# Mixer B of an encoder layer: queries sorted by class, one preparation stage, and TensorE in program order

## The chip, the cores and the metric

The kernel runs on one core of one Trainium2 chip. The metric is the device time of one execution in microseconds (us), lower is better. A core has TensorE (PE: matmuls; PEld: loads of their stationary operands), VectorE (DVE), ScalarE (ACT), GpSimdE (POOL), SyncE (SP, which here only issues transfers) and 16 DMA engines. Each engine works its own instructions off in order; semaphores tie the engines together.

## What is computed

One layer of an encoder over 1024 tokens of width 1024, in float32:

```
u = RMSNorm(x);  [qA|kA|vA|qB|kB|vB] = u @ w_in
oA = RMSNorm(global GQA of qA,kA,vA)              # mixer A, 8 query heads
oB = RMSNorm(mixture of 3 dilated windows)        # mixer B, 8 heads of 64
h = x + concat(oA, oB) @ w_out
h = h + HierarchicalMoE(RMSNorm(h))               # 32 experts
y = RMSNorm(h)

# mixer B, for window, dilation in ((128,1), (512,4), (2048,16)):
#   query t attends t + j*dilation for |j*dilation| <= window/2
#   outputs of the three are merged by their softmax denominators
```

## The kernel before

**Stages.** The input projection runs first and mixer A's attention is mixed into it; mixer A's rest follows, with the first heads of mixer B beside it; then comes mixer B, with the half of the output projection that needs only mixer A; then the other half with the router; then 32 experts one after the other; then the final norm. Expert weights stream in from HBM through 39 buffers of 512 KB ("units"), 14 of which lie where mixer B's tiles (`keep`) lay before.

**Mixer B.** Scores are kept transposed, keys on partitions and queries along the free axis. The dilations 4 and 16 are handled together by class: a class is the tokens with equal t mod 4, so there are 4 classes of 256 tokens, and each class needs two key tiles of 128 by 256 queries (`front_c`, `back_c`). The window of dilation 1 is handled in 8 key tiles of 128 by 256 queries, two per step (`front_w`, `back_w`). A head so has 8 steps. The front of a step is four matmuls into a bank of `ps_b` (keys high and low parts against queries, lines 705 and 706 for classes, 731 and 732 for windows), then `masked`: DVE adds the mask (line 691), ACT takes the exponential and rounds it to `ph`, POOL subtracts to get the low part `pl` (line 696). The back is six matmuls of the values with `ph` and `pl` (lines 718 to 721, 758 to 760), then an add into the head's output `ob` (line 762). After a head's last back `divided` transposes `ob`, divides by the denominator and writes `o_b`. In the class fronts both the keys `k2[:, ks]` (the stationary operand) and the queries `q2[:, c::4]` (the moving operand) are read with a step of four elements.

**Preparation.** Before a head's fronts its keys and queries are transposed on TensorE (`flipped`, line 303), and the row maximum of all scores is found. `prepare_b` does the flips and four class maxima (matmul line 642, DVE line 644), `finish_b` the maxima over windows (line 670, DVE line 673), brings the class maxima back to token order with four small matmuls (line 662), writes the negative maximum into the queries and flips them again to `q1`. These are two stages: while head h runs, head h+1 is finished and head h+2 prepared. Three sets of `k2`, `q2` and `q_st` are kept for it.

**Order.** `attend` writes a step as front, back of the step two before, three pieces of preparation. The output projection's first half (`first_half`, matmul line 827) advances by one piece per step. `tc` then schedules every engine by its own timeline, so that what stands on TensorE in mixer B is the scheduler's order; only the router stage and the experts hold TensorE to program order (`manual_schedule`). The first half needs the first four 128-row blocks of w_out, which come through one buffer (`raw`, line 800) and are split by ACT and DVE into `woh` and `wol`.

Of the kernel before, what the change touches and what calls it, by code (L numbers as in the profile page):

```python
# [22 lines left out]
P = 128  # L23
# [35 lines left out]
def _tables():  # L59
# [28 lines left out]

    band = []
    for j in (0, 1, 1, 7):  # L90
        near = np.abs((128 * j + p)[:, None] - (_window(j) + q)[None, :]) <= 64
        band.append(add(near.astype(int)))
# [33 lines left out]
def tile_encoder(ctx, tc, I, out):  # L126
# [171 lines left out]
    def flipped(dst, src, rows):  # L298

        for b in range(2):  # L300
            ps = bank("x", [P, 4, P], F32R)
            for i in range(4):
                T.transpose(ps[:rows, i], src[:, 4 * b + i], eyer)
            act(dst[:rows, 512 * b:512 * b + 512].rearrange("p (j i) -> p j i", j=4), ps[:rows])
            yield
# [142 lines left out]
    def attend(n, stages, steps, ahead, pace):  # L448
# [17 lines left out]
        waiting = []  # L466
        for h in range(n):
            coming = [stage(d - 1 - a, h + 1 + a) for a in range(d) if h + 1 + a < n]
            for front, back in steps(h, state.pop(h)):
                front()  # L470
# [11 lines left out]
        for back in waiting:  # L482
            back()
# [89 lines left out]
    sizes = [D] * 9 + [2 * NT * NQ, NT * NQ + 4 * P]  # L573
    keep = ExitStack()

    def spot(i):
# [3 lines left out]
    k_st, *pairs, q20 = [pools[i].tile([P, n], F32R, name=f"keep{i}") for i, n in enumerate(sizes[:-1])]  # L580
    q1b = pools[-1].tile([P, NT * NQ], F32R, name="q1b")
    back_m = pools[-1].tile([P, 4, P], F32, name="back")
    k2s = {2: pairs[0], 0: pairs[2], 1: pairs[5]}
    q2s = {2: pairs[1], 0: pairs[3], 1: pairs[6]}
    k1s = [t[0:66] for t in (pairs[4], pairs[7])]
    k_st = k_st.rearrange("p (t f) -> p t f", t=NT)
    q_st = {i: t.rearrange("p (t f) -> p t f", t=NT) for i, t in
            ((2, q20[:, 0:NT * NQ]), (0, q20[:, NT * NQ:2 * NT * NQ]), (1, q1b))}
# [6 lines left out]
    mask_c, mask_w = masks[:, 0:2], masks[:, 2:6]  # L595
    own = small[:, 60:64]
# [21 lines left out]
    def load_b(h):  # L618
        if h < 8:
            nc.sync.dma_start(k_st.bitcast(F32), bk_d[h])  # L620
            nc.sync.dma_start(q_st[h % 3][:, :, 0:192].bitcast(F32), bq_d[h])

    def prepare_b(h, _):
        k, q = k_st, q_st[h % 3]
# [7 lines left out]
        k2 = k2s[h % 3]  # L632
        yield from flipped(k2, k, P)
        q2 = q2s[h % 3]
        yield from flipped(q2, q[:, :, 0:128], P)
        load_b(h + 1)
        mc = qst2.tile([P, 4, 2], F32, name="mc", bufs=3)
# [9 lines left out]
        return k2, q2, mc  # L647

    def finish_b(h, state):
        k2, q2, mc = state  # L650
        q = q_st[h % 3]
        k1 = k1s[h % 2]
        nc.sync.dma_start(k1[0:64].bitcast(F32), k2[64:128].bitcast(F32))
        mw = qst2.tile([P, NT], F32, name="mw")
        junk = qst2.tile([P, 256], F32, name="junk", bufs=1)
# [4 lines left out]
        pm = bank("x", [P, 4, 2])  # L660
        for c in range(4):
            T.matmul(pm, back_m[:, c], mx[:, c], start=(c == 0), stop=(c == 3))
        m = qst2.tile([P, NT], F32, name="m")
        V.tensor_copy(m.rearrange("p (t i) -> p t i", t=2), pm.rearrange("p i t -> p t i"))
        yield
        for j0 in range(0, NT, 2):
# [8 lines left out]
            yield  # L675
        t = qst2.tile([P, NT], F32, name="negm")
# [5 lines left out]
        yield from flipped(q1, q[:, :, 128:194], 66)  # L682
        return k2, k1, q2, q1

    def steps_b(h, state):
# [3 lines left out]
        def masked(ps, mask):  # L689
            p = pp2.tile([P, 512], F32, name="p", bufs=2)  # L690
            V.tensor_tensor(p, ps.rearrange("p a b -> p (a b)"), mask.rearrange("p a b -> p (a b)"), op=OP.add)
            act(p, p, AF.Exp, scale=0.125)
            ph = pp2.tile([P, 512], F32R, name="ph", bufs=3)
            act(ph, p)
            pl = pp2.tile([P, 512], F32R, name="pl", bufs=3)
# [3 lines left out]
        def front_c(c):  # L699
            if c == 2:  # L700
                load_v(h, "w")
            ps = bank("b", [P, 2, 256])
            for t in range(2):
                ks = slice(512 * t + c, 512 * t + 512, 4)
                T.matmul(ps[:, t], k2[:, ks], q2[:, c::4], start=True, stop=False)
                T.matmul(ps[:, t], k1[:, ks], q1[:, c::4], start=False, stop=True)
            st["c", c] = masked(ps, mask_c)

        def back_c(c):
            if c == 0:  # L710
# [656 lines left out]
```

## Time and profile before

| | us |
|---|---|
| median of 3 runs (1396.47 to 1398.05) | 1397.87 |
| the profiled execution | 1393.38 |
| its span, which all rows below count in | 1391.7 |
| mixer B with the first half of the output projection | about 430 to 670 |
| output projection's second half, router | 670 to 780 |
| experts | 780 to 1360 |

PE is the engine that is busy nearly everywhere, and its granted clock is full except in short stretches. A matmul's duration counts its way through the array as well, so that matmuls overlap in the records; what one costs in a row of others is the distance of two starts.

### The profile page before, as it was taken

The page shows a single profiled execution, that of the slowest core. Times are in us where ns is not written, and L with a number is a line of the kernel's source. Part 1 is how long each engine was busy: PE and PEld are TensorE (multiplying, and loading weights), DVE is VectorE, ACT ScalarE, POOL GpSimd, SP SyncE. Part 2 cuts the span into 40 slices and gives each one's busy share as a digit, 9 for nine tenths or more (in the row PEclk, how much of TensorE's full clock was granted, in tenths as well). Part 3 has the DMA queues.
Part 4 walks back from the last instruction along what each step waited for, and adds up shares of the span by engine and source line. Part 5 has one row for each costly group of instructions (what it writes and reads, how often), then busy time and mean ns, then how long its engine had stood idle before and what let it go on. Part 6 is the DMA issues. An engine that isn't in the chain of part 4 may idle for free. (4 is left out here: it accounts for less than half of the span.)

```text
span 1391.7 us, 21904 instructions
## 1 busy us (share of the span) xinstructions
PE 1303.2 (94%) x7333; PEld 1110.6 (80%) x7333; DVE 1152.4 (83%) x2001; ACT 926.2 (67%) x1366; POOL 568.6 (41%) x556
## 2 busy tenths in 40 slices
PE   5999899999998999999897999999999999999983
PEld 5999779888976889889686788878888888888862
DVE  5788997899868777667587799989999999999976
ACT  5334556655566656556443688878888888888873
POOL 5673566745566645446354611122111111111215
PEclk9999999999998999899998999999999999999997
DMA  7113321231242564445767999999999999999925
GB/s 258 62 39 85 84 68 54 61 75 36 58 138 60 145 186 117 112 128 164 278 210 240 308 371 367 353 341 372 360 351 351 345 360 355 349 353 342 376 74 226
DMA packets 213044, 299.63 MB, mean 215 GB/s; under 512 B 94307, under 2 KB 115939, under 8 KB 212928
## 3 DMA queue, kind: packets, MB, share of 16 engines
q1 hardware_dynamic: 200528, 272.91, 58.1%
q0 software_dynamic: 11968, 24.55, 6.7%
q8 instruction: 58, 0.95, 0.3%
q10 hardware_dynamic: 432, 0.75, 0.3%
q14 instruction: 58, 0.48, 0.1%
HBM read 267.85 MB, written 44.58 MB: 224 GB/s over the span
## 5 line engine op out<-in xcount | busy, mean ns | idle before, releaser
L140 DVE TENSOR_TENSOR wl<-unit,wh 128x1024 fp32r<-128x1024 f32 x140 | 168.4, 1223 | 21.1 <-ACT wh L131 20.1
L1163 POOL DMA_INDIRECT o_b<-xn_d,rows x32 | 51.4, 1606 | 303.1 <-PE ps_a L1180 300.8
L131 ACT ACTIVATE wh<-unit 128x1024 fp32r<-128x1024 f32 x140 | 147.3, 1062 | 36.3 <-PE ps_b L1196 12.5
L529 POOL TENSOR_TENSOR psum<-psum,p 128x512 f32<-128x512 f32 x93 | 138.0, 1484 | 66.7 <-ACT p L131 56.6
L263 PE MATMUL ps_i<-wih,ul 128*128 128x256 f32 x576 | 163.1, 283 | 1.2 <-DVE ul L140 1.2
L261 PE MATMUL ps_i<-wih,uh 128*128 128x256 f32 x576 | 162.7, 283 | 0.8 <-ACT uh L131 0.8
L262 PE MATMUL ps_i<-wil,uh 128*128 128x256 f32 x576 | 162.2, 282 | 0.0
L131 ACT ACTIVATE ph<-p 128x512 fp32r<-128x512 f32 x192 | 119.0, 630 | 12.7 <-DVE pl L445 5.7
L445 DVE TENSOR_TENSOR pl<-p,ph 128x512 fp32r<-128x512 f32 x93 | 96.1, 1035 | 24.7 <-ACT ph L131 24.6
L131 ACT ACTIVATE p<-ps_b 128x512 f32<-128x512 f32 x128 | 74.6, 595 | 62.2 <-PE ps_b L519 39.7
L261 PEld LDWEIGHTS ps_i<-wih,uh 128*128 128x128 f32 x576 | 109.6, 190 | 7.0 <-ACT uh L131 1.5
L262 PEld LDWEIGHTS ps_i<-wil,uh 128*128 128x128 f32 x576 | 109.4, 190 | 5.5
L263 PEld LDWEIGHTS ps_i<-wih,ul 128*128 128x128 f32 x576 | 109.5, 190 | 5.1 <-DVE ul L140 1.7
L696 POOL TENSOR_TENSOR pl<-p,ph 128x512 fp32r<-128x512 f32 x64 | 83.4, 1309 | 73.2 <-ACT ph L131 51.9
L1233 POOL DMA_INDIRECT y_d<-y,rows x31 | 50.3, 1622 | 137.5 <-ACT y L131 134.2
L140 DVE TENSOR_TENSOR wl<-rawc,wh 128x1024 fp32r<-128x1024 f32 x70 | 84.4, 1223 | 10.4 <-ACT wh L131 9.9
L500 DVE TENSOR_REDUCE m<-ps_x 128x1 f32<-128x512 f32 x128 | 84.9, 678 | 7.9 <-PE ps_x L499 7.6
L1196 PE MATMUL ps_b<-wh,x_hi 128*128 128x512 f32 x256 | 87.0, 421 | 0.0
L131 ACT ACTIVATE wh<-rawc 128x1024 fp32r<-128x1024 f32 x70 | 74.3, 1067 | 18.2 <-PE ps_b L1196 7.2
L1220 PE MATMUL ps_d<-wh,h_hi 128*128 128x512 f32 x256 | 81.0, 397 | 1.7 <-ACT h_hi L131 1.7
L1220 PE MATMUL ps_d<-wh,h_lo 128*128 128x512 f32 x256 | 81.1, 398 | 1.5 <-DVE h_lo L140 1.5
L1196 PE MATMUL ps_c<-wh,x_hi 128*128 128x512 f32 x256 | 80.9, 397 | 0.0
(326 smaller groups left out, 3888.9 us busy)
## 6 DMA issues: line engine op xcount, KB each, us to landing
unit<-in_w_up SPq DMA_DIRECT2D x49, 512.0 KB
unit<-in_w_gate SPq DMA_DIRECT2D x47, 512.0 KB
unit<-in_w_down SPq DMA_DIRECT2D x44, 512.0 KB
rawc<-in_w_gate SPq DMA_DIRECT2D x25, 512.0 KB
rawc<-in_w_down SPq DMA_DIRECT2D x23, 512.0 KB
rawc<-in_w_up SPq DMA_DIRECT2D x22, 512.0 KB
h_b<-in_w_down SPq DMA_DIRECT2D x19, 512.0 KB
raw<-in_w_in SPq DMA_DIRECT2D x36, 256.0 KB
```

Of the source, the lines that this page charges most:

```text
L131: A.activation(o, i, f, **kw)
L140: (eng or V).tensor_tensor(lo, src, hi, op=OP.subtract)
L261: T.matmul(ps[:, jj], u_hi[j][:, k], wh, start=(k == 0 and jj == 0), stop=False, skip_group_check=True)
L262: T.matmul(ps[:, jj], u_hi[j][:, k], wl, start=False, stop=False, skip_group_check=True)
L263: T.matmul(ps[:, jj], u_lo[j][:, k], wh, start=False, stop=(k == 7), skip_group_check=True)
L445: engine("pl").tensor_tensor(pl, p, ph, op=OP.subtract)
L500: V.tensor_reduce(m2[:, j, b:b + 1], ps, axis=AX.X, op=OP.max)
L529: engine("s").tensor_tensor(st["s"], st["s"], p, op=OP.add)
L696: G.tensor_tensor(pl, p, ph, op=OP.subtract)
L1163: gathers.append(G.indirect_dma_start(out=x_g, out_offset=None, in_=xn_d[:, :], in_offset=bass.IndirectOffsetOnAxis(ap=rows, axis=0), boun ...
L1196: T.matmul(st["gu"[n % 2]], lhs[:, k % 4], rhs[:, 512 * a:512 * a + 512], start=(k == 0 and i == 0), stop=(k == 7 and i == 2))
L1220: T.matmul(py[b], lhs[:, k], w[n][:, 512 * b:512 * b + 512], start=(k == 0 and i == 0), stop=(k == 3 and i == 2))
```

## The change

Four things change, in mixer B and in what is mixed into it.

1. **Queries by classes.** After its flip, `q2` is copied by ACT into `q2c` with the four classes one after another (`classes`, `by_class`), and `q1` is flipped straight into that order. Class fronts read 256 queries that lie together; window fronts read four blocks of 64. The window masks, `ps` and `po` follow the same order, so that the DVE maxima over windows read their bank with a step of four, and the add into `ob` reads and writes `ob` with a step of four. The keys as stationary operand are read as before, and so are both operands of the class maxima.
2. **One stage.** `prepare_b` and `finish_b` become one; there are two sets of `k2`, `q2c`, `k1`, one `q2`, two `q_st`. The four small matmuls stand after the window maxima, and three empty pieces stand ahead of the flip of `q1`. The copy of `k2` to `k1` is issued right after the flip of `k2`. Eleven instead of 14 units lie where those tiles lay.
3. **More distance.** The back runs three steps after its front instead of two; `p` has 3 buffers, `ph` and `pl` have 4; `divided` runs some parts after the last back; the values of the windows are loaded one step later.
4. **TensorE by the program.** `attend(..., fine=True)` yields after every part (front, piece, back, piece, piece); the output projection advances once in 4.2 parts; the whole loop stands under `manual_schedule` for TensorE, while the other engines are scheduled as before. In `first_half` the norm of the next row (`normed`) and its transposes (`turned`) are apart.

```
-    def flipped(dst, src, rows):
+    def flipped(dst, src, rows, classed=False):
...
+            if classed:
+                act(classes(dst[:rows])[:, :, 128 * b:128 * b + 128], by_class(ps[:rows].rearrange("p j i -> p (j i)")))
...
+                if fine:
+                    waiting.append(back)
...
+                    def second():
+                        if len(waiting) > ahead:
+                            owing.extend([3, f] for f in waiting.pop(0)() or ())
+
+                    for part in (front, piece, second, piece, piece)[:2 + pace]:
+                        part()
+                        for o in owing:
+                            o[0] -= 1
+                        if owing and owing[0][0] < 0:
+                            owing.pop(0)[1]()
+                        yield
+                    continue
...
+        q2c = q2s[h % 2]
+        act(classes(q2c), by_class(q2))
...
-                V.tensor_tensor_reduce(junk, ps[:, t], mask_w[:, w], 1.0, NEG, op0=OP.add, op1=OP.max,
-                                       accum_out=mw[:, j0 + t:j0 + t + 1])
+                V.tensor_tensor_reduce(classes(junk), by_class(ps[:, t]), classes(mask_w[:, w]), 1.0, NEG,
+                                       op0=OP.add, op1=OP.max, accum_out=mw[:, j0 + t:j0 + t + 1])
...
+        for _ in range(3):
+            yield
+        yield from flipped(q1, q[:, :, 128:194], 66, True)
+        return k2, k1, q2c, q1
...
-            p = pp2.tile([P, 512], F32, name="p", bufs=2)
+            p = pp2.tile([P, 512], F32, name="p", bufs=3)
...
-                T.matmul(ps[:, t], k2[:, ks], q2[:, c::4], start=True, stop=False)
-                T.matmul(ps[:, t], k1[:, ks], q1[:, c::4], start=False, stop=True)
+                T.matmul(ps[:, t], k2[:, ks], q2[:, 256 * c:256 * c + 256], start=True, stop=False)
+                T.matmul(ps[:, t], k1[:, ks], q1[:, 256 * c:256 * c + 256], start=False, stop=True)
...
-                    V.tensor_tensor(o[:, b0:b0 + nb], o[:, b0:b0 + nb], po[0:65, 0:nb], op=OP.add)
+                    V.tensor_tensor(by_class(o[:, b0:b0 + nb]), by_class(o[:, b0:b0 + nb]), po[0:65], op=OP.add)
...
-    side = attend(8, [prepare_b, finish_b], steps_b, 2, 3)
+    side = attend(8, [prepare_b], steps_b, 3, 3, True)
...
+    with tc.manual_schedule(engines={mybir.EngineType.PE}):
+        for _ in side:
+            due += RATE_O / 4.2
```

TensorE around the first steps of a head, before: `L642` are class maxima, `L705` and `L706` class fronts, `L718` and `L720` a back.

```order
L642 MATMUL ps_x<-keep_5000,keep_5001 128x256 x2
L706 MATMUL ps_b<-q_5822,keep_5007 128x256
L705 MATMUL ps_b<-keep_5006,keep_5005 128x256
L706 MATMUL ps_b<-q_5822,keep_5007 128x256 x2
...
L718 MATMUL ps_i_6113<-ph,v_c 65x256
L720 MATMUL ps_i_6113<-ph,v_c 64x256
```

The same place after (`L678` class maxima, `L692` window maxima, `L735` and `L736` class fronts, `L789` to `L791` a back, `L861` the output projection, `L853` its transposes).

```order
L735 MATMUL ps_b<-keep_4999,keep_4998 128x256
L736 MATMUL ps_b<-q_5813,keep_5000 128x256
L735 MATMUL ps_b<-keep_4999,keep_4998 128x256
L736 MATMUL ps_b<-q_5813,keep_5000 128x256
L861 MATMUL ps_d<-woh,o_hi 128x512
L861 MATMUL ps_d<-wol,o_hi 128x512
L861 MATMUL ps_d<-woh,o_lo 128x512
L678 MATMUL ps_x<-keep_4995,keep_4994 128x256 x2
L789 MATMUL ps_i_6035<-ph,v_w 65x4x64
```

Where three class fronts stood in one row, one front is now followed by a product of the output projection, a maximum and a back.

TensorE at the end of mixer B, before: `L740` is `divided`, `L819` the transposes of the first row of the second half, `ps_x` the bank of its products.

```order
L827 MATMUL ps_d<-woh,o_lo 128x512
...
L740 MATMUL ps_i_8109<-mats,ob 128x65 x4
L740 MATMUL ps_i_8118<-mats,ob 128x65 x4
L819 MATMUL ps_b<-mats,on 128x128 x4
L827 MATMUL ps_x<-woh,o_hi 128x512
```

And after (`L770` is `divided`, `L853` those transposes):

```order
L791 MATMUL ps_i_8115<-pl,v_w 65x4x64
L770 MATMUL ps_i_8123<-mats,ob 128x65 x4
L770 MATMUL ps_i_8132<-mats,ob 128x65 x4
L861 MATMUL ps_d<-woh,o_hi 128x512
L861 MATMUL ps_d<-wol,o_hi 128x512
L861 MATMUL ps_d<-woh,o_lo 128x512
...
L853 MATMUL ps_b<-mats,on 128x128 x4
```

Five groups of three products of the first half now stand between the last division and those transposes; ahead of the division the backs of the last four steps stand, in four sixes, with one group of products after the first of them.

ScalarE in the preparation of a head, after: `p` and `ph` are the exponentials and their rounding, `keep_4994` is `q2`, `keep_4999` is `q2c`.

```order
L132 ACTIVATE keep_4994<-ps_x 128x512
L132 ACTIVATE ph<-p 128x512
L132 ACTIVATE keep_4994<-ps_x 128x512
L132 ACTIVATE p<-p 128x512
L132 ACTIVATE keep_4999<-keep_4994 128x1024
L132 ACTIVATE ph<-p 128x512
```

The copy of 1024 elements is new and stands between an exponential and its rounding.

## Rows read from the trace of the kernel before

**Rows 1.** The page: busy time by engine; granted clock in 40 slices.
```profile
PE 1303.2 (94%) x7333; PEld 1110.6 (80%) x7333; DVE 1152.4 (83%) x2001; ACT 926.2 (67%) x1366; POOL 568.6 (41%) x556
...
PEclk9999999999998999899998999999999999999997
```

**Rows 2.** Stretches from:to: length, busy us (instructions), granted clock, DMA share; mixer B, experts.
```profile
430.00:670.00 240.00, 229.39 (x1406) 206.28 (x1404) 173.79 (x497) 149.42 (x255) 123.85 (x118) 0.93 0.48 131
...
780.00:1360.00 580.00, 572.76 (x2639) 462.40 (x2637) 520.55 (x506) 482.18 (x564) 118.41 (x85) 1.00 0.96 337
```

**Rows 3.** The same view: one of six half-clock stretches of mixer B, and their sum.
```profile
575.10:585.40 10.30, 10.30 (x54) 9.88 (x54) 5.20 (x19) 6.34 (x12) 4.81 (x4) 0.50 0.21 45
...
sum 37.60, PE 37.14 PEld 34.68 DVE 23.38 ACT 21.40 POOL 18.12; mean PE 6.19 PEld 5.78 DVE 3.90 ACT 3.57 POOL 3.02
```

**Rows 4.** The same view: the longest stretch between two of these.
```profile
493.20:551.20 58.00, 55.45 (x352) 49.39 (x352) 43.76 (x122) 33.97 (x60) 25.29 (x28) 1.00 0.54 146
```

**Rows 5.** Timeline of PE, start us, us: class fronts before the clock fell at 575.1.
```profile
574.85 0.42 PE L706 MATMUL ps_b<-q,keep 66*128 66x256 f32 x1
575.08 0.43 PE L705 MATMUL ps_b<-keep,keep 128*128 128x256 f32 x1
575.32 0.42 PE L706 MATMUL ps_b<-q,keep 66*128 66x256 f32 x1
...
576.45 0.41 PE L718 MATMUL ps_i<-ph,v_c 128*65 128x256 f32 x1
576.66 0.41 PE L720 MATMUL ps_i<-ph,v_c 128*64 128x256 f32 x1
```

**Rows 6.** Timeline, all engines: window fronts at full clock.
```profile
585.62 0.28 PE L731 MATMUL ps_b<-keep,keep 128*128 128x256 f32 x1
...
585.74 0.29 PE L732 MATMUL ps_b<-q,keep 66*128 66x256 f32 x1
```

**Rows 7.** Timeline of PEld: two loads each; L670's operand lies together, L642's is stepped.
```profile
585.99 0.31 PEld L670 LDWEIGHTS ps_x<-keep,keep 128*128 128x128 f32 x2
...
587.96 0.55 PEld L642 LDWEIGHTS ps_x<-keep,keep 128*128 128x128 f32 x2
```

**Rows 8.** Groups by line in 430:670: count | busy us, mean ns | idle before, releaser.
```profile
L691 DVE TENSOR_TENSOR p<-ps_b,masks 128x512 f32<-128x512 f32 x64 | 43.9, 686 | 14.5 <-PE ps_b L706 7.4 <-POOL pl L696 4.4 <-PE ps_b L732 2.6
...
L705 PE MATMUL ps_b<-keep,keep 128*128 128x256 f32 x64 | 29.0, 453 | 3.0 <-DVE p L691 2.9
L673 DVE CUSTOM_DVE_ANT_0 junk<-ps_x,masks 128x256 f32<-128x256 f32 x64 | 26.9, 421 | 14.9 <-PE ps_x L670 12.9 <-PE ps_b L519 0.5
...
L131 ACT ACTIVATE ob<-ps_i 65x512 f32<-65x512 f32 x16 | 17.6, 1098 | 6.9 <-PE ps_i L721 6.7
...
L642 PEld LDWEIGHTS ps_x<-keep,keep 128*128 128x128 f32 x62 | 17.0, 322 | 0.5
L131 ACT ACTIVATE keep<-ps_x 128x512 fp32r<-128x512 f32 x28 | 16.5, 596 | 7.5 <-PE ps_x L303 7.3
...
L762 DVE TENSOR_TENSOR ob<-ob,ps_i 65x448 f32<-65x448 f32 x8 | 4.9, 607 | 0.0
```

**Rows 9.** Waits of PE in 430:670: us in total, times, longest.
```profile
PE ps_b L705 <- DVE p L691: 2.9, 2, 1.6
...
PE ps_x L662 <- DVE mx L658: 1.0, 2, 0.5
```

**Rows 10.** Timeline of PE at the end of mixer B.
```profile
669.68 0.47 PE L740 MATMUL ps_i<-mats,ob 65*128 65x65 f32 x4 [0.35 <-DVE ob L762]
672.68 0.66 PE L819 MATMUL ps_b<-mats,on 128*128 128x128 f32 x4 [2.54 <-DVE on L814]
...
676.69 0.80 PE L827 MATMUL ps_x<-woh,o_lo 128*128 128x512 f32 x1 [1.50 <-DVE o_lo L140]
```

**Rows 11.** Timeline of ACT: splits of the third and fourth block of w_out.
```profile
499.33 1.06 ACT L131 ACTIVATE woh<-raw 128x1024 fp32r<-128x1024 f32 x1 [1.00 <-DMA raw<-in_w_out]
505.48 1.05 ACT L131 ACTIVATE woh<-raw 128x1024 fp32r<-128x1024 f32 x1
```

More of the change, by code (lines that the diff above doesn't have):

```diff
@@ L91, in _tables @@
         near = np.abs((128 * j + p)[:, None] - (_window(j) + q)[None, :]) <= 64
-        band.append(add(near.astype(int)))
+        band.append(add(near.astype(int)).reshape(P, 64, 4).transpose(0, 2, 1).reshape(P, 256))
     masks = np.stack(cls + band, 1)
@@ L446, in weights, with attend @@
         return ph, pl
-    def attend(n, stages, steps, ahead, pace):
+    def attend(n, stages, steps, ahead, pace, fine=False):
         state, at = {}, {}
@@ L482, in attend @@
         for back in waiting:
-            back()
+            owing.extend([0, f] for f in back() or ())
+        for _, f in owing:
+            f()
     qst = att.enter_context(tc.tile_pool(name="qst", bufs=2))
@@ L579, in tile_encoder @@
     pools = [keep.enter_context(spot(i)) for i in range(len(sizes))]
[L580 to L585, printed above, removed]
+    k_st, q2, *pairs, q01 = [pools[i].tile([P, n], F32R, name=f"keep{i}") for i, n in enumerate(sizes)]
+    k2s, q2s, k1s = pairs[0::3], pairs[1::3], [t[0:66] for t in pairs[2::3]]
     k_st = k_st.rearrange("p (t f) -> p t f", t=NT)
-    q_st = {i: t.rearrange("p (t f) -> p t f", t=NT) for i, t in
-            ((2, q20[:, 0:NT * NQ]), (0, q20[:, NT * NQ:2 * NT * NQ]), (1, q1b))}
+    q_st = [q01[:, i * NT * NQ:(i + 1) * NT * NQ].rearrange("p (t f) -> p t f", t=NT) for i in range(2)]
     final = {}
@@ L672, in finish_b @@
                 w = 0 if j0 + t == 0 else 3 if j0 + t == NT - 1 else 1
-                V.tensor_tensor_reduce(junk, ps[:, t], mask_w[:, w], 1.0, NEG, op0=OP.add, op1=OP.max,
-                                       accum_out=mw[:, j0 + t:j0 + t + 1])
+                V.tensor_tensor_reduce(classes(junk), by_class(ps[:, t]), classes(mask_w[:, w]), 1.0, NEG,
+                                       op0=OP.add, op1=OP.max, accum_out=mw[:, j0 + t:j0 + t + 1])
             yield
+        pm = bank("x", [P, 4, 2])
+        for c in range(4):
+            T.matmul(pm, back_m[:, c], mx[:, c], start=(c == 0), stop=(c == 3))
+        yield
+        m = qst2.tile([P, NT], F32, name="m")
+        V.tensor_copy(m.rearrange("p (t i) -> p t i", t=2), pm.rearrange("p i t -> p t i"))
         t = qst2.tile([P, NT], F32, name="negm")
@@ L854, in first_half @@
                 V.tensor_tensor(h[:, j], ps, x[b], op=OP.add)
+                if b == 0 and j + 1 < NT:
+                    o = turned(on, "x")
+                yield
         split_out(4)
@@ L858, in tile_encoder @@
     more, due = first_half(), 0.0
-    for _ in side:
-        due += RATE_O
-        while due >= 1:
-            due -= 1
-            next(more, None)
-    run(more)
+    with tc.manual_schedule(engines={mybir.EngineType.PE}):
+        for _ in side:
+            due += RATE_O / 4.2
+            while due >= 1:
+                due -= 1
+                next(more, None)
+        run(more)
     names.update(a="b", b="x", c="d", d="i1", s="i0")
-    first_mixed = turned(o_b[0][:, 0], 1, "a")
+    first_mixed = turned(normed(o_b[0][:, 0], 1), "a")
     wka.close()
```

91 lines of the change are left out of this document (46 added, 45 removed).

## Prediction

> **What bounds the kernel now.** I read the page first, then the stretches, then inside mixer B the groups by line, the timeline and the waits. The page says that PE is busy for 94% of the span and that its clock is full but for some slices in the middle [rows 1]. In the experts PE is busy for 573 of 580 us at full clock [rows 2], so what is won or lost before them moves the end by about as much; the change touches nothing there. The work that changes lies in 430 to 670. There PE is busy for 229 of 240 us, but the clock is 0.93, and DVE is the second engine with 174 us, 72% [rows 2]. [...] PE's own waits are small: for a free bank `ps_b` 2.9 us, for the row maxima 1.0 [rows 9]. The tail is larger: from the last division at 669.68 to 676.69 PE waits 2.54 and 1.50 us for the norm of the first row of the next stage [rows 10]. So mixer B is nearly bound by PE, with DVE not far behind, and what can be won is the stepped reading, the half clock, these waits and the tail.
>
> **The change part by part.** All against the profiled execution of 1393.4 us; the median of the runs is 4.5 higher, which I add at the end.
>
> 1. *Queries that lie together.* 128 matmuls (L705 has 64 [rows 8], L706 as many) now have a moving operand without a step; their stationary operand, the keys, is stepped as before. If only the moving operand sets 0.235, they fall to 0.12: 128 x 0.115 = 14.7 us. But loads of stepped stationary operands are slow too: two take 0.55 together [rows 7] and one of them lasts 0.32 [rows 8], so the second starts some 0.22 behind the first; two that lie together take 0.31 [rows 7]. Four fronts in a row are then paced by their loads at 0.22. That gives 128 x 0.015 = 2 us, and a little more where the first load of a four hides behind the matmul ahead. I take -3 us, between 0 and -15.
>
> 2. *Clock.* At half clock a back's matmuls start 0.21 apart (576.45 to 576.66 [rows 5]) instead of about 0.12; stepped ones lose nothing. By counts, half clock does 54 matmuls in 10.3 us, 5.2 per us [rows 3], full clock 352 in 58, 6.1 per us [rows 4]: 37.6 us at the lower rate lose some 5 us; if nothing in them were stepped, half, 19. I hold 10 for near. In the new order a front stands between products of 512 columns and a back, so the long runs of slow columns that stood ahead of the fall are gone; the class maxima keep their steps, and new waits (5) may let the clock fall again. I take half of it back: -5, between 0 and -14.
>
> 3. *Waits that the new order is made around.* The maxima come back to token order after the window maxima, the flip of `q1` after three empty pieces, and the back a step later. The two waits, 2.9 + 1.0 = 3.9 us [rows 9], should nearly go: -3.5, between 0 and -3.9. What is late next is DVE.
>
> 4. *Tail.* Five groups of three products stand between the last division and the transposes of the next row; at 580 us / 2639 = 0.22 us each [rows 2] they are 3.3 us, which cover most of 2.54 + 1.50 [rows 10]. -3.5, between -2 and -4.
>
> 5. *TensorE in program order beside DVE.* The scheduler could put other matmuls ahead of one whose bank was not free; now PE waits. A head's eight maxima each cost DVE two instructions of 0.42 [rows 8], 0.84 us, and PE 0.24 to 0.47. They stand three to a step over about two and two thirds steps, beside the masks (0.69 a step [rows 8]), two adds of 0.6 [rows 8], the divisions and an add of the output projection: some 12 us of DVE against 10 us of PE. The three banks of `ps_x` let PE run ahead by about one piece; the rest, 1 us or a little more for each of seven heads, PE stands still, and behind the waiting matmul a front stands, and so ACT and POOL. +7, between 0 and +14.
>
> 6. *Stepped reading by DVE and ACT.* 64 maxima over windows read their bank with a step of four, 24 adds into `ob` read and write with it, ACT has one more copy of 1024 a head and reads the bank of `q1` with a step. No row shows DVE with a step. The nearest are the ACT writes of `ob` with a step of four, 1098 ns for 512, against 596 for `keep` without [rows 8]: 1.0 ns an element more. By that a maximum would cost 0.26 us more, 64 x 0.26 = 17 us of DVE just where (5) has it behind, and the adds 24 x 0.43 = 10 us. On the other side PE reads with the step at 0.235 / 256 = 0.92 ns an element, about as fast as a maximum takes its elements anyway (0.42 us for 256), so a read may cost nothing. I take reads at nothing and writes at the price of `ob`: 10 us of DVE spread over 24 places, where DVE is idle 28% of the time; a tenth shows, +1. The copy, 1.1 to 2.1 us of ACT a head by the same rows, lies behind fronts with three steps of slack: 0. Together +1, between 0 and +27.
>
> [...]
>
> 7. *w_out.* Its blocks pass one buffer, and the splits of the third and fourth stand 6.15 us apart (499.33, 505.48 [rows 11]). In program order the products that need blocks 2 to 4 stand two to four us apart on PE and can't be passed by other work. If the chain of loads starts as before, PE waits 2 to 6 us once, less what it would have waited for DVE anyway. +2, between 0 and +6.
>
> 8. *The rest at nothing:* the empty pieces, the copy to `k1` earlier on SP, the values of the windows a step later but used four steps after their load as before, the larger rings, and eleven early units, which like the fourteen fill while the router stage runs. If those came late, the first expert would wait, and DMA share above 0.96 [rows 2] shows that there is little to catch up with.
>
> Sum: -3 - 5 - 3.5 - 3.5 + 7 + 1 + 2 = -5 on 1393.4, so 1388.4, and with 4.5 added 1392.9. Items 2 and 5 are both rough, and a program order that is steady on PE lessens small losses that I priced nowhere: starts in 430 to 670 that come late by less than what the waits list. I give these 2.9 us more and forecast 1390.
>
> **The rivals.** *The gains all come:* the clock stays up (-14), the loads hide (-8), tail and waits go and DVE keeps pace (+2): about -25, 1373. For it: the falls came behind slow runs; against it: DVE at 72% has to do the same in less time. *Nothing:* the scheduler had hidden the stepped reading, the program order loses as much at DVE as it wins; 1398. That the change doesn't do what it says belongs here: the keys keep their step, and class fronts stay at 0.22. *Slower:* DVE pays for the step in PSUM. 64 maxima at +0.26 are 17 us in the place where PE waits for banks: 1390 - 1 + 17 = 1406. It decides from about +0.13 us each, where the gain is gone. For it: the `ob` rows; against it: PE's 0.92 ns.
>
> **How the numbers follow.** Forecast (1382 to 1394) 0.42, all gains (1366 to 1382) 0.19, nothing 0.16, slower (1401 to 1412) 0.23. A measurement of this kernel can tell about 0.2%, 2.8 us, from no change. Faster so is 0.42 + 0.19 = 0.61, same 0.16, slower 0.23. The range takes the forecast, nothing, most of the gains and the nearer half of the slower case: 1370 to 1406.
>
> **What would show it.** In the profile after: starts of class fronts 0.21 to 0.22 apart (near 0.12 says that loads don't count, 0.235 that nothing changed). Less than 25 us at half clock in mixer B; as much as before says that item 2 is wrong. A maximum over windows at 0.42 as before, or 0.55 and more, which is the slower rival. PE's waits for DVE on `ps_x` of 5 to 10 us in sum. Transposes of the next stage's first row within 1.5 us of the products ahead of them. First products of w_out with waits of some us for `woh`. The forecast falls if mixer B and the first half of the output projection don't end some 6 us earlier, or if the experts then wait for weights.

## The result, and the profile after

The changed kernel takes 1416.33 us, median of 4 runs (1412.85 to 1422.50); the kernel before 1397.17 in the same series. The ratio is 1.0152, 95% interval 1.0126 to 1.0178: some 21 us slower, where 1390 was forecast and 1406 was the upper end of the range. The profiled run took 1415.44 us.

First the page: span, PE's busy time, and the granted clock in 40 slices, to be laid beside [rows 1].
```profile
span 1413.8 us, 21932 instructions
...
PE 1310.6 (93%) x7333; PEld 1114.0 (79%) x7333; DVE 1162.6 (82%) x2001; ACT 942.3 (67%) x1374; POOL 565.7 (40%) x556
...
PEclk9999999999997699989999899999999999999997
```
The number of matmuls is the same. The thirteenth and fourteenth slice (424 to 495 us) stand at 0.7 and 0.6 where they stood at 0.8 and 0.9 before: mixer A ends there and mixer B begins in earnest. The stretches say the same, after and then before (from:to, length, busy us (instructions) of PE, PEld, DVE, ACT, POOL, clock, DMA share, GB/s):
```profile
428.00:470.00 42.00, 35.17 (x157) 26.23 (x157) 26.61 (x59) 27.41 (x48) 23.77 (x17) 0.78 0.13 38
470.00:505.00 35.00, 29.05 (x150) 26.32 (x150) 24.02 (x57) 19.14 (x32) 15.64 (x16) 0.66 0.54 146
...
560.00:620.00 60.00, 55.39 (x344) 50.60 (x343) 41.10 (x120) 37.41 (x61) 26.04 (x26) 0.91 0.43 111
...
428.00:698.00 270.00, 237.94 (x1414) 210.14 (x1415) 185.69 (x506) 164.88 (x267) 126.55 (x126) 0.89 0.43 118
...
800.00:1380.00 580.00, 572.83 (x2634) 463.29 (x2633) 521.30 (x507) 481.88 (x564) 116.80 (x81) 1.00 0.96 338
```
```profile
428.00:470.00 42.00, 39.20 (x220) 33.48 (x221) 31.87 (x84) 29.51 (x54) 27.02 (x20) 0.88 0.18 47
470.00:505.00 35.00, 32.27 (x210) 28.67 (x207) 27.20 (x75) 24.64 (x43) 18.84 (x20) 0.90 0.70 181
...
560.00:620.00 60.00, 56.49 (x341) 51.34 (x341) 41.17 (x128) 33.37 (x58) 27.42 (x27) 0.91 0.44 114
```
From 428 to 505 PE does 307 instructions where it did 430. The last division of mixer B begins at 690.19, 20.5 us behind [rows 10]; the two spans differ by 22.1. Nine groups of three products of the first half still stand behind it, where before the last of them had started at 667.98. So the first product of the second half starts at 698.99 instead of 674.02; the experts run as in [rows 2]. PE's timeline after, then before:
```profile
690.19 0.46 PE L770 MATMUL ps_i<-mats,ob 65*128 65x65 f32 x4 [0.56 <-DVE ob L793]
...
695.14 0.60 PE L853 MATMUL ps_b<-mats,on 128*128 128x128 f32 x4
...
698.99 0.39 PE L861 MATMUL ps_x<-woh,o_hi 128*128 128x512 f32 x1
```
```profile
674.02 0.73 PE L827 MATMUL ps_x<-woh,o_hi 128*128 128x512 f32 x1 [0.69 <-ACT o_hi L131]
```

PE's waits between 428 and 692 (us in sum, times, longest) have changed their kind. Over 428 to 698 they sum to 31.9 us against 15.4 before, 4.7 of which lie behind 670 in the next stage [rows 10]. The longest sums after:
```profile
PE ps_x L312 <- DVE keep L708: 5.9, 5, 1.9
PE ps_x L692 <- DVE mw L695: 4.2, 5, 1.6
PE ps_i L746 <- issue: 3.6, 2, 2.3
PE ps_d L573 <- DVE pl L457: 3.2, 6, 0.8
PE ps_x L700 <- DVE mw L695: 2.9, 3, 1.8
PE ps_d L861 <- ACT o_hi L132: 1.9, 1, 1.9
```
L312 is the flip of `q1`, which needs the negative maximum (L708); L692 a product whose bank a maximum (L695) still reads; L746 the first back of a class, L573 mixer A's back, L700 the product that brings the maxima to token order. The wait of [rows 9] for a free `ps_b`, 2.9 us, is gone. Behind such a wait the clock falls in some cases and not in others. In PE's timeline the wait of 1.61 us ends at 599.54, and the stretch from 599 to 611 has a clock of 0.57 (the nine us ahead: 1.00):
```profile
597.52 0.40 PE L692 MATMUL ps_x<-keep,keep 128*128 128x256 f32 x2
599.54 0.58 PE L692 MATMUL ps_x<-keep,keep 128*128 128x256 f32 x2 [1.61 <-DVE mw L695]
```
```profile
599.00:611.00 12.00, 10.57 (x50) 9.62 (x51) 7.37 (x25) 5.07 (x9) 2.84 (x5) 0.57 0.18 46
```
In slices of 1 us from 428 to 698 the changed kernel's clock is 0.50 in 56, 1.00 in 206 and between the two in 8. Four of the five half-clock stretches after begin within 2.5 us of the start of a wait (waits from 447.2, from 465.7 on, from 514.0 and from 597.9); the longest, 466 to 494, is 28 us at 0.51, and the waits ahead of it were of 0.2 to 0.6 us. Waits of 1.3 to 1.9 us that ended at 498, 571, 636 and 662 had no fall behind them. So the waits go with the falls in part; that they cause them is not shown.

The groups by line of the changed kernel, beside [rows 8] (count | busy us, mean ns | idle before):
```profile
L736 PE MATMUL ps_b<-q,keep 66*128 66x256 f32 x64 | 25.5, 399 | 0.0
L735 PE MATMUL ps_b<-keep,keep 128*128 128x256 f32 x64 | 25.0, 391 | 0.3 <-ACT p L132 0.3
...
L695 DVE CUSTOM_DVE_ANT_0 junk<-ps_x,masks 128x256 f32<-128x256 f32 x64 | 26.8, 419 | 2.9 <-PE ps_x L692 1.8
...
L132 ACT ACTIVATE keep<-keep 128x1024 fp32r<-128x1024 f32 x7 | 14.6, 2085 | 0.0
...
L793 DVE TENSOR_TENSOR ob<-ob,ps_i 65x448 f32<-65x448 f32 x8 | 8.0, 998 | 1.8 <-PE ps_i L791 1.1 <-ACT ph L132 0.7
```
The maximum over windows reads its bank with a step of four and takes 419 ns, against 421 without. So the mechanism of my slow rival did not come; the kernel is slower for another reason. The add into `ob` does pay for its step, 998 against 607. And class fronts in PE's timeline, at full clock, still start 0.23 to 0.24 apart. The four below are among the nine, of 29 fours in a row at full clock, whose first two start 0.12 apart; the median of the first distance is 0.23 as well:
```profile
641.52 0.28 PE L735 MATMUL ps_b<-keep,keep 128*128 128x256 f32 x1
641.63 0.39 PE L736 MATMUL ps_b<-q,keep 66*128 66x256 f32 x1
641.86 0.40 PE L735 MATMUL ps_b<-keep,keep 128*128 128x256 f32 x1
642.10 0.39 PE L736 MATMUL ps_b<-q,keep 66*128 66x256 f32 x1
```

### The profile page after: what moved, and what is told of

It is laid out like the page before. It is cut to its first block, busy times and chain, and to the rows that moved or that the text cites. A ratio compares the mean times of both kernels' runs of the same rounds, so it can differ in the third digit from the quotient of the medians.

```text
span 1413.8 us, 21932 instructions
## 1 busy us (share of the span) xinstructions
PE 1310.6 (93%) x7333; PEld 1114.0 (79%) x7333; DVE 1162.6 (82%) x2001; ACT 942.3 (67%) x1374; POOL 565.7 (40%) x556
## 5 line engine op out<-in xcount | busy, mean ns | idle before, releaser
L141 DVE TENSOR_TENSOR wl<-unit,wh 128x1024 fp32r<-128x1024 f32 x110 | 132.6, 1224 | 17.6 <-ACT wh L132 16.8
L132 ACT ACTIVATE wh<-unit 128x1024 fp32r<-128x1024 f32 x110 | 115.8, 1062 | 29.8 <-PE ps_b L1235 10.7
L141 DVE TENSOR_TENSOR wl<-rawc,wh 128x1024 fp32r<-128x1024 f32 x100 | 120.3, 1223 | 13.5 <-ACT wh L132 13.1
L132 ACT ACTIVATE wh<-rawc 128x1024 fp32r<-128x1024 f32 x100 | 105.4, 1063 | 25.0 <-PE ps_b L1235 10.1
L1235 PE MATMUL ps_b<-wl,x_hi 128*128 128x512 f32 x256 | 81.6, 400 | 0.0
```

What stands on the lines that cost most here:

```text
L132: A.activation(o, i, f, **kw)
L141: (eng or V).tensor_tensor(lo, src, hi, op=OP.subtract)
L1235: T.matmul(st["gu"[n % 2]], lhs[:, k % 4], rhs[:, 512 * a:512 * a + 512], start=(k == 0 and i == 0), stop=(k == 7 and i == 2))
```

## The experiments

All differences in us are differences of the ratios to the kernel before, times 1393 (the kernel before had medians of 1391.5 to 1394.4 in these series). Each ratio's interval is given once, in the table; a difference of two is uncertain by some 3 to 7 us. "Waits" are PE's, in sum, and the clock is the mean, both between 428 and 698 of one profiled run, a window that holds a little more of the next stage in a faster kernel. The profiled run of e2 is the fastest of its ten (1392.3 us), so its waits and clock are those of a good run. "Order" says whether PE follows the program in mixer B; "whole" whether mixer B is advanced by whole steps while mixer A ends; "empty" counts the pieces between the maxima and the flip.

| kernel | order | whole | empty | us | ratio (95%) | waits | clock |
|---|---|---|---|---|---|---|---|
| before | no | yes | - | 1397.2 | 1 | 15.4 | 0.92 |
| changed | yes | no | 3 | 1416.3 | 1.0152 (1.0126 to 1.0178) | 31.9 | 0.89 |
| e1 | yes | yes | 3 | 1414.8 | 1.0142 (1.0111 to 1.0172) | 31.0 | 0.87 |
| e2 | no | no | 3 | 1401.8 | 1.0050 (1.0026 to 1.0074) | 24.0 | 0.94 |
| e4 | no | yes | 3 | 1387.6 | 0.9959 (0.9942 to 0.9976) | 19.2 | 0.95 |
| e5: e4, no classes | no | yes | 3 | 1392.8 | 0.9997 (0.9971 to 1.0023) | 17.1 | 0.89 |
| e6: e1, maxima spread | yes | yes | 1 | 1423.8 | 1.0244 (1.0210 to 1.0278) | 37.6 | 0.87 |
| e7: e1, banks not held | yes | yes | 3 | 1428.1 | 1.0270 (1.0245 to 1.0296) | 40.3 | 0.86 |
| e8: before, with order | yes | yes | - | 1415.3 | 1.0178 (1.0127 to 1.0228) | 29.7 | 0.88 |
| e9: e4, maxima spread | no | yes | 1 | 1396.4 | 1.0035 (1.0015 to 1.0054) | 21.2 | 0.90 |
| e10: order, last 4 heads | part | yes | 3 | 1404.5 | 1.0087 (1.0052 to 1.0121) | 28.6 | 0.90 |
| e11: order, first 3 heads | part | yes | 3 | 1402.1 | 1.0058 (1.0025 to 1.0091) | 30.2 | 0.89 |
| e12: e4, bank by steps | no | yes | 3 | 1384.9 | 0.9939 (0.9912 to 0.9967) | 18.1 | 0.95 |
| e13: e1, products first | yes | yes | 3 | 1441.0 | 1.0317 (1.0281 to 1.0353) | 36.4 | 0.83 |
| e14 | yes | yes | 8 | 1398.5 | 1.0026 (1.0002 to 1.0051) | 26.0 | 0.96 |
| e15: e12, denser | no | yes | 6 | 1393.1 | 0.9994 (0.9976 to 1.0013) | 21.4 | 0.94 |
| e16: e7, no order | no | yes | 3 | 1416.3 | 1.0130 (1.0090 to 1.0170) | 36.5 | 0.89 |
| e17 | yes | no | 8 | 1429.6 | 1.0223 (1.0183 to 1.0262) | 37.6 | 0.87 |
| e18 | no | yes | 8 | 1398.9 | 1.0012 (0.9989 to 1.0036) | 22.3 | 0.93 |
| e19: e12 with order | yes | yes | 6 | 1404.9 | 1.0078 (1.0045 to 1.0110) | 25.5 | 0.93 |

### Order and cover, one by one and together (e1, e2, e4), and the classes (e5)

The comparison of the traces gave a suspect that the prediction had not seen. In the changed kernel `attend` yields five times a step (`fine`), but the loop over mixer A's rest still takes one `next(side)` a turn. Ahead of mixer A's last instruction, at 477, stand 115 of mixer B's in PE's record before, and 40 after. e1 hands out whole steps there:
```diff
+    whole = []
     def attend(n, stages, steps, ahead, pace, fine=False):
...
-                        yield
+                        if not whole:
+                            yield
+                    if whole:
+                        yield
...
+    whole.append(1)
     for _ in turns:
         next(side, None)
+    whole.clear()
```


> The changed kernel (1416.3 us), but while mixer A's rest runs, mixer B is advanced by a whole step a turn (front, three pieces, one back) once its first head is prepared, not by a fifth of one; the order of TensorE in mixer B stays that of the program. Theory A (the end of mixer A lost its cover: 40 instead of 115 TensorE instructions of mixer B stand before mixer A's last one, 75 x 0.17 = 13 us): 1400 to 1406 us, and over 90 of them stand there. Rival B (the waits inside TensorE's fixed order cost it all along): 1412 or more. Rival C (the classes' extra work on VectorE and ScalarE) and rival D (one stage instead of two): within 4 us of 1416.

e2 takes out the order, and e4 has both edits:
```diff
-    with tc.manual_schedule(engines={mybir.EngineType.PE}):
-        for _ in side:
+    for _ in side:
```


> The changed kernel, but TensorE in mixer B is given out by the scheduler again and not in the order of the program. Theory A (lost cover at the end of mixer A): the scheduler may draw work of mixer B forward past mixer A's last products, 1396 to 1404 us. Rival B (waits in the fixed order all along): 1390 to 1397, with the PE's waits for VectorE on ps_x in mixer B back under 10 us in sum. Rivals C and D (classes, one stage): 1410 or more.

> Both edits: whole steps during mixer A's rest and TensorE by the scheduler. Theory A: within 4 us of the better of the two single edits (each gives back the same cover). Rival B: 12 us or more under the kernel that has whole steps alone. Rivals C and D: 1408 or more.

The cover came back in e1 (111 instructions ahead of mixer A's last), and the time did not: 1414.8. Theory A as I put it fell. Under the scheduler the same edit is worth 13 us (e2 to e4), and the order costs 14 us without it and 25 with it. The stretches of e1, then of e4, show where e1's cover goes: what was done earlier by 470 is lost again by 505, and later stretches lose too.
```profile
428.00:470.00 42.00, 39.09 (x212) 33.71 (x211) 31.90 (x86) 32.20 (x55) 24.79 (x18) 0.85 0.18 49
470.00:505.00 35.00, 25.56 (x133) 23.02 (x133) 24.70 (x66) 18.11 (x30) 16.73 (x16) 0.72 0.60 147
560.00:620.00 60.00, 55.63 (x315) 50.12 (x313) 39.36 (x116) 35.62 (x56) 23.84 (x24) 0.83 0.39 106
```
```profile
428.00:470.00 42.00, 37.10 (x209) 31.03 (x209) 32.12 (x83) 31.83 (x53) 23.76 (x17) 0.89 0.17 48
470.00:505.00 35.00, 29.36 (x198) 27.29 (x197) 29.64 (x82) 24.84 (x40) 22.89 (x21) 0.90 0.64 150
560.00:620.00 60.00, 58.05 (x401) 54.14 (x399) 46.02 (x139) 40.23 (x65) 26.19 (x26) 1.00 0.51 131
```
e5 puts plain queries, masks and adds back into e4:
```diff
-                T.matmul(ps[:, t], k2[:, ks], q2[:, 256 * c:256 * c + 256], start=True, stop=False)
+                T.matmul(ps[:, t], k2[:, ks], q2[:, c::4], start=True, stop=False)
...
-        act(classes(q2c), by_class(q2))
```


> As the kernel with both edits, but the queries, the window masks, the window's outputs and the add into ob are in the plain order as in the kernel before, and the copy of the queries by classes is gone; one stage of preparation stays. Rival C (the classes cost: 24 adds into ob at +0.4 us, 8 copies at about 1.1 us, in all 18 us of VectorE and ScalarE): 6 us or more faster than with classes. If the classes are worth what TensorE saves on them (about 8 us of full-pace work): 4 to 8 us slower than with classes. Theory A says nothing here; rival D (one stage): 1405 or more with or without classes.

So the classes are worth 5 us (some 1 to 10 by the two intervals), in spite of their adds and copies, and rival C fell. One stage instead of two, with `fine` and the other small parts, costs nothing in sum: e5 stands at 0.9997 of the kernel before, so D fell too.

### What the order costs, and where (e8, e10, e11)

e8 is the kernel before with nothing but the `with tc.manual_schedule` line of the change.

> The kernel before, with two stages, plain queries and whole steps, and one thing alone: TensorE in mixer B in the order of the program. If the fixed order costs by itself: 1405 to 1425 us, slower than before by at least 10. If it costs only together with one stage (whose maxima stand close before the flip that needs them): 1392 to 1402.

It costs 25 us there (18 to 32 by the interval): neither classes nor one stage are needed for it. Its largest waits of PE:
```profile
PE ps_x L303 <- DVE keep L680: 5.6, 4, 1.5
PE ps_i L760 <- POOL pl L696: 4.9, 7, 1.2
PE ps_i L740 <- DVE ob L762: 3.9, 8, 1.6
PE ps_x L303 <- DVE q1b L680: 3.9, 2, 3.0
```
The flips again, but backs and divisions as well: other places, as many us. e10 and e11 put a part of e4's loop in order:
```diff
+    for _ in itertools.islice(side, 120):
...
+    with tc.manual_schedule(engines={mybir.EngineType.PE}):
+        for _ in side:
```


> Whole steps during mixer A's rest and TensorE by the scheduler (1387.6 us), but the last 160 of the loop's 280 parts (from the fourth of its seven heads on, roughly from 560 us) in program order. Theory S (the fixed order costs at its start, where mixer A has just ended and the clock stood at 0.66 to 0.85 from 470 to 560 us, and hardly where it was 1.00 after 620): 1386 to 1393. Rival X (it costs alike everywhere): 1387.6 + 27 x 160/280 = 1403, so 1399 to 1407.

> The complement: the first 120 parts (three heads) in program order, the other 160 by the scheduler. Theory S: 1408 to 1416. Rival X: 1387.6 + 27 x 120/280 = 1399, so 1395 to 1403.

Four heads in order cost 18 us, three cost 14, all seven 25 (e1): some 4 us a head, in the first half as in the second. The start is not special (theory S fell), though the clock is lowest there.

### Which wait it is (e6, e7, e16, e13, e14, e17, e18, e19)

e6 takes the maxima apart, in the hope that VectorE frees the banks of `ps_x` in time (the output projection then advances once in 3.36 parts):
```diff
-        for _ in range(3):
-            yield
+        yield
...
-    side = attend(8, [prepare_b], steps_b, 3, 3, True)
+    side = attend(8, [prepare_b], steps_b, 3, 2, True)
```


> TensorE in program order and whole steps during mixer A's rest (1414.8 us), but two pieces of the preparation a step instead of three, and one empty piece instead of three, so that the 18 maxima and flips of a head lie over all eight of its steps. Theory W (in the fixed order TensorE stands at the ps_x banks that VectorE's maxima hold, 13 us of waits, and the clock falls after them, 18 us): half of both goes, 1398 to 1405 us, and the waits for mc and mw fall under 6 us in sum. Rival X (any fixed order of these chains loses, wherever the maxima stand): 1411 or more.

It lost 14 us more. The flip now stands one piece behind the last maximum, and PE's waits at the flip alone rose to 16.4 us:
```profile
PE ps_x L312 <- DVE keep L713: 16.4, 7, 3.7
```
e9 is the same under the scheduler:

> Whole steps, TensorE by the scheduler (1387.6 us), and the preparation spread over all eight steps as in the other kernel. Theory W: the scheduler already goes past held banks, so 1384 to 1391. If the density of the maxima costs by VectorE's queue and not by TensorE's order: 1378 to 1383.

It loses 11 us there as well, so the late maxima, with the flip close behind them, cost in either order. In e7 no bank of `ps_x` waits for a maximum; the kernel leaves the true maxima out:
```diff
-                V.tensor_tensor_reduce(junk, ps[:, t], mask_c[:, t], 1.0, NEG, op0=OP.add, op1=OP.max,
+                V.tensor_tensor_reduce(junk, mask_w[:, t], mask_c[:, t], 1.0, NEG, op0=OP.add, op1=OP.max,
...
-                V.tensor_tensor_reduce(classes(junk), by_class(ps[:, t]), classes(mask_w[:, w]), 1.0, NEG,
+                V.tensor_tensor_reduce(classes(junk), by_class(mask_c[:, t]), classes(mask_w[:, w]), 1.0, NEG,
```


> TensorE in program order and whole steps (1414.8 us), but VectorE's maxima read the masks and not the product in ps_x: as many of the same size, and no bank of ps_x waits for VectorE there (the maximum subtracted before the exponential is then another constant, which the division takes out again). The flips that need the maximum wait as before. Theory W: 1396 to 1404 us, with no wait for mc or mw left. Rival X: 1410 or more, other waits in their place.

> The maxima read the masks and not the banks of ps_x, as in the kernel with program order (1428.1 us), here with TensorE by the scheduler. There the maxima took 709 to 785 ns in place of 420, which by itself costs. Theory W (the fixed order costs by the held banks of ps_x): with free banks the order costs nothing, 1422 to 1430. Theory G (it costs by waits in every chain): 1398 to 1406, so that the order costs its 27 us without any held bank.

The pair has longer maxima than meant (means of 785 and 709 ns in e7, 777 and 716 in e16, against 419 in the changed kernel; more below), so each is slow; but the order still costs 12 us by the medians and 20 by the ratios, with no wait for a held bank of `ps_x` left. PE's longest waits in e7:
```profile
PE ps_x L312 <- DVE keep L713: 10.1, 4, 4.7
PE ps_d L578 <- DVE pl L457: 8.0, 5, 3.5
PE ps_i L751 <- issue: 5.6, 3, 3.1
```
So theory W fell for the most part of the price; that the held banks are the rest, 5 to 13 of the 25 us, is not ruled out. e13 gives the output products out where the wait for the flip is:
```diff
         for _ in range(3):
+            want.append(4)
             yield
...
-            due += RATE_O / 4.2
-            while due >= 1:
-                due -= 1
-                next(more, None)
+            while want:
+                for _ in range(want.pop()):
+                    next(more, None)
```


> TensorE in program order and whole steps (1414.8 us), but the output products (12 to a block, they wait for nothing of mixer B) are not given out three at a time at even distances: 36 of them stand in the three empty pieces between the last maximum and the flip that needs it, as the scheduler puts 10 to 12 of them together. Theory F (under the scheduler these products fill the long waits, and the fixed order spreads them where nothing waits): the wait of the flips goes (4.5 us) and with it a part of the clock's fall, 1398 to 1408. Theory G (the waits are many and short and sit in every chain, so no one place of the products mends them): 1411 to 1418.

It is the slowest of all. The flip still waits 5.4 us, and the first backs of a class wait 11.0, with no releaser that the view names:
```profile
PE ps_i L752 <- issue: 11.0, 6, 4.4
PE ps_x L312 <- DVE keep L713: 5.4, 2, 3.5
```
The record of PE shows what the scheduler does instead: between 470 and 690 the kernel before has the products in runs of 1 to 12 (seven runs of twelve, four of ten, eight of two), the changed kernel in 55 runs of three. It puts them where PE would stand, a different place in each head; one fixed place is worse than an even spread. e14 makes the way to the flip longer:
```diff
-        for _ in range(3):
+        for _ in range(8):
             yield
         yield from flipped(q1, q[:, :, 128:194], 66, True)
```


> TensorE in program order and whole steps (1414.8 us), with eight empty pieces in place of three between the maxima and the flip that needs them. If the flip's wait (4.5 us, and the clock after it) is the main price: 1403 to 1409, with waits for the negative maximum under 1 us. Theory G: 1411 to 1418, the wait moves to the fronts that need the flipped rows (ScalarE's copy).

16 us faster than e1, more than the flip's waits (4.5 us) held. Its clock is 0.96 where e1 had 0.87; 0.09 x 2 x 270 is 49 us less at half clock, though only 5 us less of waits (e14, then e1):
```profile
428.00:698.00 270.00, 243.80 (x1507) 214.73 (x1508) 196.29 (x537) 172.45 (x288) 130.91 (x135) 0.96 0.52 148
```
```profile
428.00:698.00 270.00, 239.27 (x1408) 214.53 (x1407) 186.04 (x510) 163.82 (x266) 126.12 (x127) 0.87 0.45 123
```
Is it that distance that the changed kernel lacks, and only in the fixed order? e17 is the changed kernel with this edit alone, e18 is e4 with it:

> The changed kernel (1416.3 us) with one edit alone: eight empty pieces in place of three before the flip; fixed order, and mixer B advanced by a fifth of a step a turn while mixer A ends. Theory D (the flip's wait in the fixed order, and the fall of the clock behind it, is the largest part of the loss; with whole steps the edit gave back 16 us): 1399 to 1406 us. If the edit only works with whole steps: 1410 or more.

> Whole steps, TensorE by the scheduler (1387.6 us), eight empty pieces in place of three. Theory D: the scheduler passes the flip by anyway, so the distance is worth little here, 1384 to 1391; the gain of 16 us belongs to the fixed order. If the distance is worth the same without it: 1372 to 1380.

Both misses tell something. Under the scheduler the edit costs 7 us, so that with eight empty pieces the order costs 2 us, within the error. But in the changed kernel the edit costs 10 us. The new waits there, of PE in e17:
```profile
PE ps_b L736 <- ACT q L132: 7.1, 7, 1.9
PE ps_x L692 <- DVE mc L680: 6.7, 7, 1.7
PE ps_x L692 <- DVE mw L695: 4.5, 4, 1.4
```
The fronts now wait for ScalarE's copy of the flipped rows, once a head. The empty pieces also delay the first head while mixer A ends: 28 of mixer B's instructions are ahead of mixer A's last (40 in the changed kernel, 50 in e14). But that is not where e17 lost: the last division of its first head starts at 513.37, in the changed kernel at 513.58, and the seven heads behind it take 192.7 us against 176.6, and 169.3 in e14. Why they do is not shown. e19 sets six, with e12's add:

> Program order, whole steps, six empty pieces (between three, 1414.8 us, and eight, 1398.5 us, where the fronts waited 6 us for the flipped rows), and the add into ob by steps of the bank (worth 2.7 us under the scheduler). Theory D: 1391 to 1398 us, the waits for the negative maximum and for the flipped rows both under 3 us. If six is still too near: 1400 to 1408.

1404.9, between e1 and e14, and 19 us above e12, which is the same but for the order and three empty pieces.

### A better kernel (e12, e15)

e12 walks the add in plain order: `ob` in SBUF contiguous, the step in PSUM.
```diff
-                    V.tensor_tensor(by_class(o[:, b0:b0 + nb]), by_class(o[:, b0:b0 + nb]), po[0:65], op=OP.add)
+                    os = o[:, b0:b0 + nb].rearrange("p (i c) -> p i c", c=4)
+                    V.tensor_tensor(os, os, po[0:65].rearrange("p c i -> p i c"), op=OP.add)
```


> Whole steps and TensorE by the scheduler, and the add into ob goes through the columns in plain order: ob in SBUF contiguous, the bank of PSUM by steps, the same sum. If steps cost VectorE in SBUF alone (the window maxima by steps in PSUM took 420 ns against 424): the 448-column adds fall from 1001 to 600 to 700 ns, the waits for ob behind them (5.1 us) by half, 1378 to 1386 us. If the price is that of any step: still about 1000 ns, 1386 to 1390.

The 448-column add, in e12 and then in e4:
```profile
L799 DVE TENSOR_TENSOR ob<-ob,ps_i 65x448 f32<-65x448 f32 x8 | 4.9, 613 | 0.5 <-PE ps_i L796 0.3
```
```profile
L798 DVE TENSOR_TENSOR ob<-ob,ps_i 65x448 f32<-65x448 f32 x8 | 7.7, 963 | 0.6 <-PE ps_i L796 0.3
```
The price of the step is gone. The time fell by 2.8 us, which the intervals do not separate from nothing. At 0.9939 of the kernel before e12 is the fastest: classes, whole steps, PE by the scheduler. A denser preparation on top of it did not help:

> Whole steps, TensorE by the scheduler, the add into ob by steps of the bank (1384.9 us), with four pieces a step instead of three and six empty ones before the flip: the maxima stand earlier in the head. If the spread kernel lost its 9 us because the maxima came too late for the next head: 1376 to 1384. If the scheduler takes it as it comes: 1383 to 1388. If VectorE's queue in the first half of a head is the limit: 1388 to 1395.

It lost 8 us; the maxima in a row crowd VectorE or come too early, or the six empty pieces cost by themselves (eight cost 7 us in e18), which is not told apart here.

## Why the prediction was wrong

Two steps failed: the program order was priced at 7 us and cost 14 to 25, and the loop that advances mixer B while mixer A ends, worth 13 us, had no term at all. By the prediction's items:

- **Queries together** (-3): right in mechanism. Fronts start 0.23 apart at full clock as at half (I had 0.22, against 0.235 by the starts of [rows 5] and 0.12 by those of [rows 6]), though their queries now lie together; the window fronts of the changed kernel, whose keys lie together as well, start 0.12 apart there. The loads differ in the same way: they last 322 to 328 ns with stepped keys, 215 to 217 without. All of the classes together, with item 6, were worth -5 (e5 to e4), where I had -2; which part of them brings it is not shown.
- **Clock** (-5): wrong in sign. 0.89 against 0.92 over 270 us is 16 us more at half clock, not 19 less; by the mean clock of every run it is 16 as well (117 us of the span over 4 runs after, 101 over 87 runs before). I had laid the falls to slow runs of columns and said that the classes would take those away; the falls of the changed kernel stand beside waits. Two of the six of [rows 3], at 486.4 and 619.5, also began within 1 us behind the two waits of [rows 9] for `ps_b`, which I had not set beside each other. With the order taken out the clock is 0.95 with classes (e4) and 0.89 without (e5) in the profiled runs, but over ten runs of each the two differ by only 8 us at half clock (98 and 106): a part of the gain was there to be had.
- **Known waits** (-3.5): the wait for `ps_b` went, but the one for the token order grew from 1.0 to 2.9 us, and the flip's came to 5.9. The three empty pieces did not cover the way.
- **Tail** (-3.5): right. The transposes of the next row follow the products with no wait, and 0.8 + 0.4 us of others are left of the 4.0 of [rows 10]. The products that cover the wait stood ahead of the last division before.
- **Program order** (+7, 0 to +14): the term that was mis-sized most. It costs 14 us here (e2), 25 in e1 and in the kernel before (e8), some 4 us a head. I priced one kind of wait, the held banks, at 1 us a head. The runs show that banks, flips, class backs and fronts all wait, and that mending one moves a part of it to another. With eight empty pieces the order costs 2 us (e14 against e18), but e14 still stands 9 us behind e4.
- **Stepped reading** (+1): reads of PSUM free (419 ns against 421) and adds at +0.39 us, as taken; the copy at 2085 ns, the upper end; the adds come to some 3 us by e12, within the error.
- **w_out** (+2): did not come. No product of the first half waits for a block; the first waits 1.9 us for `o_hi`.
- **A steady order** (-2.9, taken off the sum at the end): I gave the program order a gain that no row showed. The opposite came: from e4 to e1 PE's waits rise from 19.2 to 31.0 us.
- **Missing:** the loop that advances mixer B while mixer A ends. The change cuts a step into five parts, and the diff leaves that loop at one a turn. I had no term for it; it is worth 13 us under the scheduler.

From the kernel before to the changed one by runs: nothing for one stage and the rest (e5), -5 for the classes (e4), +13 for the lost cover (e2), +14 for the order. The last two depend on each other: taken the other way round the order costs 25 first (e1), and then the cover nothing more (+1). A kernel that loses time by the order has no use for the cover.

Of the rivals, "slower" had the right side and a mechanism that did not exist. "Against it: PE's 0.92 ns" was the better evidence.

**Open** stays how the order's price divides between waits and clock: no run held the clock while leaving the waits, and e5 has the changed kernel's clock of 0.89 with 17 us of waits and 1392.8 us. The record allows an estimate. Each run has its span and mean clock; if the clock is 0.50 or 1.00, as in 262 of the 270 slices of 1 us above, its time at half clock is 2 x (1 - clock) x span, and among runs of the same kernel one us more at half clock goes with about 0.3 us of time (0.33 over the 87 runs of the kernel before). From e4 to e1 the mean over the runs rises from 98 to 118 us at half clock, which is some 6 of the 25 us; from e1 to e14 it falls to 92, some 8 of the 16, so that the 49 us of the two profiled runs overstate it. By this estimate the larger part of the order's price is not the clock. Open too is why eight empty pieces gain in e14 and lose in e17.

## What to carry to other kernels

A scheduler that may pass a waiting matmul by was worth up to 25 us here, and 2 us, within the error, once the flip stood eight pieces behind its maxima. Before an engine's order is fixed, count each chain's way through the other engines in that engine's work, for every wait and not only the one that is listed now. When a generator is cut into finer parts, look for every loop that counts its parts. And where a layout has to be stepped on VectorE, put the step on the operand in PSUM: here the add of 448 columns took 613 ns so (e12), and 963 with the step in SBUF (e4).

## What the runs showed of the hardware

- VectorE read PSUM with a step of four elements at the price of none: the maximum over 256 took 419 ns in the changed kernel and 421 without the step in the kernel before, the add of 448 columns 613 in e12 and 607 in the kernel before. With `ob` in SBUF read and written by that step the add took 963 in e4 and 998 in the changed kernel.
- ScalarE's copies of the flipped rows to `q`, most of which read their bank with a step of four in the changed kernel, took 585 ns for 66x512 against 588 before; its copy of 1024 with the step in SBUF took 2085, where one without (`wh` from `unit`, the kernel before) took 1062.
- A maximum whose two inputs are both in SBUF (e7) took 424 ns in the median, or 622 with a step, but up to 1667 and 1672, where with one input in PSUM (e1) none took over 433:
```profile
L700 DVE CUSTOM_DVE_ANT_0 junk<-masks x64: 591/622/1667, 430.4 to 622.9; 128x256 f32<-128x256 f32 x64
L685 DVE CUSTOM_DVE_ANT_0 junk<-masks x58: 390/424/1672, 429.4 to 601.3; 128x256 f32<-128x256 f32 x58
```
What made some of them so long is not shown.
